# Two-block transformer kernel: the subtractions that split the modulation sums go from GpSimd to VectorE, half of an input split goes from VectorE to ScalarE, and the probabilities of differential attention are transposed one step later

## The chip, the cores and the metric

The kernel runs on one core of a Trainium2 chip. The metric is the device time of one launch in microseconds (us). Five engines work beside each other, each through its own queue in order: TensorE (PE in the profile, with its weight loads as PEld), VectorE (DVE), ScalarE (ACT), GpSimd (POOL) and SyncE (SP), which issues the transfers. An instruction that waits holds up all that stands behind it in its engine's queue.

## The reference, cut to what matters

The reference takes 256 tokens of 1024 features in fp32 through a first block (a SwiGLU feed-forward, a mixing layer of retention and neighbourhood attention, a second SwiGLU) and then through a second block of two layers. What the change touches lies in the second block:

```
mod = jnp.einsum('bd,lde->lbe', jax.nn.silu(c), ada_w) + ada_b[:, None, :]
for i in range(DEPTH_2):
    shift1, scale1, gate1, shift2, scale2, gate2 = jnp.split(mod[i], 6, axis=-1)
    h = x * (1.0 + scale1) + shift1
    y = moba_attention(h, ...) if i == 0 else diff_attention(h, ...)
    x = layer_norm(DEEPNORM_ALPHA * x + (1.0 + gate1) * y, ...)
    h = x * (1.0 + scale2) + shift2
    y = jnp.square(jax.nn.relu(h @ w_up)) @ w_down
    x = layer_norm(DEEPNORM_ALPHA * x + (1.0 + gate2) * y, ...)
# diff_attention, per head:  w = softmax(q1 k1^T) - lam * softmax(q2 k2^T);  o = rms_norm(w @ v)
```

`mod` is 12 vectors of 1024 numbers (two layers, six each). They depend on `c` alone and can be summed long before they are used.

## The kernel before, in words

**Weights as a stream.** All products with weights are made in fp32 precision from three products of a narrower form: a weight tile `raw` is split into an upper part `wh`, copied by ScalarE (L115), and a rest `wl = raw - wh`, subtracted by VectorE (L93). A pair of tiles is a slot of the stream, one tile of 128x1024 a piece. `tick` (L403 to L430) is called after each piece that TensorE has used up; it splits the next piece or two and then advances the background generators (`bg`), each of which runs up to its next `yield n` and sleeps n ticks. A generator's place on each engine's queue is thus fixed when the program is written. The stream keeps at most eight split pieces and six raw ones; SyncE's transfers are issued in the order of the stream.

**Modulation sums.** The weight `ada_w` comes as pieces of the same stream; the slots behind which they stand come from the table `at` (L310 to L314). Each of the 12 sums takes eight steps on VectorE (L335, L338) into `adacc`; partitions are not yet summed. Then `ada_parts` (L345 to L357) splits the sum into three bf16 parts: ScalarE copies (L348), GpSimd subtracts (L350), ScalarE copies (L352), GpSimd subtracts (L354). When the parts are there, `spare` sums them over the partitions by small matmuls in a PSUM bank that the hidden layer leaves free.

**Inputs.** `turn_of` (L584 to L608) transposes the normalized input on TensorE, scales and shifts it on ScalarE (`hf`, L602), and splits it on VectorE: an upper part (L606, listed as CAST) and the rest (L607). It is called for the first 128 tokens (t = 0) and the second (t = 1). While TensorE works on columns of the first, VectorE goes on to normalize the second (L646 to L659).

**Attention.** `attention.pair` is the generator of a head: scores `as` on TensorE, exponentials `P` on ScalarE (L1253), for layer 1 the difference of the two softmaxes on VectorE (L1263 to L1267), then the transposition `at` (L1276), its copy `T` on ScalarE (L1277), the product `ao` with the values, the head's norm `o` (L1308 to L1314) and its transposition (L1318). Rotation of q and k (L1223 to L1227) is emitted from the same ticks.

Of the kernel before, what the change touches and what calls it, by code (L numbers as in the profile page):

```python
# [9 lines left out]
F32 = mybir.dt.float32  # L10
F32R = mybir.dt.float32r
BF16 = mybir.dt.bfloat16
AF = mybir.ActivationFunctionType
OP = mybir.AluOpType
# [157 lines left out]
def block_kernel(ctx, tc, A, out):  # L172
    nc = tc.nc
    V, SC, PE, GP = nc.vector, nc.scalar, nc.tensor, nc.gpsimd
# [4 lines left out]
    work = ctx.enter_context(tc.tile_pool(name="work", bufs=1))  # L179
# [113 lines left out]
    for l, (wi, wo) in enumerate((("moba_w_in", "moba_w_out"), ("diff_w_in", "diff_w_out"))):  # L293
# [5 lines left out]
        for i in range(4):  # L299
# [6 lines left out]
    adas = [(l, s, i) for l, s in ((0, 0), (0, 1), (0, 3), (0, 4), (1, 0), (0, 2), (0, 5), (1, 1), (1, 3), (1, 4), (1, 2),  # L306
                                   (1, 5)) for i in range(4)]
    at = {}
    o = 0
    for n, g in ((nffn, 3), (nmix, 2), (nffn, 3), (natt, 0), (nmlp, 3), (natt, 0), (nmlp, 1)):  # L310
        for i in range(4 * g):
            a = 6 if o else 10
            at.setdefault(o + a + int((i // 4 + 0.2 * (i % 4)) * (n - a - 5) / g), []).append(adas.pop(0))
        o += n  # L314
    assert not adas
    for n, w in enumerate(ws):
# [28 lines left out]
    def ada_parts(l, s, t):  # L345

        parts = [adap[-1].tile([128, D], BF16, name=f"ada{i}", bufs=1) for i in range(3)]
        SC.activation(parts[0], t, AF.Copy)  # L348
        yield 1
        GP.tensor_tensor(t, t, parts[0], OP.subtract)  # L350
        yield 2
        SC.activation(parts[1], t, AF.Copy)  # L352
        yield 1
        GP.tensor_tensor(parts[2], t, parts[1], OP.subtract)  # L354
        yield 2
        ada_now.clear()
        ada_out.append((l, s, parts, None if s in (2, 5) else 0))  # L357

# [220 lines left out]

    def squares(s, src):  # L580

        SC.activation(work.tile([128, 512], F32, name="junk"), src, AF.Square, accum_out=s)

    def turn_of(src, a, c, alloc=gu):  # L584

        def turn(t):
            ps = [alloc("xt"), alloc("xt")]
            for k in range(8):
                PE.transpose(ps[k // 4][:, k % 4 * 128:k % 4 * 128 + 128], src[:, t, k * 128:(k + 1) * 128], ident)
            if c is None:  # L590
                for i in range(4):
                    for b in range(2):
                        k = 4 * b + i
                        x, h, l = ps[b][:, i * 128:(i + 1) * 128], XX[:, k, 0, TS[t]], XX[:, k, 1, TS[t]]
                        SC.activation(h, x, AF.Copy, scale=a[:, k:k + 1])
                        V.scalar_tensor_tensor(l, x, a[:, k:k + 1], h.bitcast(F32), op0=OP.mult, op1=OP.subtract)  # L596
                return
            for b in range(2):
                f = w2("hf")
                for i in range(4):  # L600
                    k = 4 * b + i
                    SC.activation(f[:, i * 128:(i + 1) * 128], ps[b][:, i * 128:(i + 1) * 128], AF.Identity,  # L602
                                  scale=a[:, k:k + 1], bias=c[:, k:k + 1])
                h, l = (XX[:, 4 * b:4 * b + 4, i, TS[t]] for i in range(2))
                f = f.rearrange("p (k s) -> p k s", k=4)
                V.tensor_copy(h, f)  # L606
                V.tensor_tensor(l, f, h.bitcast(F32), OP.subtract)  # L607
        return turn  # L608

# [605 lines left out]
    def attention(l, turn, after, mid):  # L1215
        with tc.tile_pool(name=f"att{l}", bufs=1) as mp:
# [13 lines left out]
            def pair(j, q, k):  # L1230
# [20 lines left out]
                for a in range(2):  # L1251
                    for c, sl in ((0, slice(0, 128)), (1, slice(128, 384))):
                        SC.activation(P[:, a, sl], ps[a][:, sl], AF.Exp, bias=mx[:, a, c:c + 1], scale=0.125,  # L1253
                                      accum_out=ss[:, c, a:a + 1])
# [5 lines left out]
                else:  # L1260
# [5 lines left out]
                    for c, sl in ((0, slice(0, 128)), (1, slice(128, 384))):  # L1266
                        V.scalar_tensor_tensor(P[:, 0, sl], P[:, 1, sl], lr[:, c:c + 1], P[:, 0, sl],  # L1267
                                               op0=OP.mult, op1=OP.add)
                yield 1
                nh = 2 - l  # L1270
                yield from room(nh)
                T = mp.tile([128, nh, 384], F32, name="T", bufs=2 + l)
# [211 lines left out]
```

## Time and profile before

| | |
|---|---|
| median of 3 runs | 1317.36 us (1317.07 to 1321.57) |
| the profiled execution's own time | 1319.84 us |
| its span, first to last instruction | 1318.0 us |
| TensorE busy | 1258.1 us, 95% |
| VectorE busy | 932.2 us, 71% |
| ScalarE busy | 642.8 us, 49% |
| GpSimd busy | 94.6 us, 7% |
| mean granted TensorE clock | 0.983 of full speed |

An execution takes 1.84 us more than its span. The stages in order are: FFN1 from about 8 to 210 us, the mixing layer to 440, FFN2 to 650, the first attention to 775, the first MLP to 965, differential attention to 1112, and the second MLP to the end. In the rows below, a line such as L93 is a line of the kernel before; a number in brackets is how long the engine idled ahead of the instruction, and what ended that; "x2" are two instructions of a kind in one row, with the time from the start of the first to the end of the last.

### The profile page before, as it was taken

The numbers are of one execution on the slowest core, as the hardware profiler recorded it, in microseconds if no ns is written. First come the engines' busy times: TensorE is split into PE (matmuls) and PEld (weight loads), VectorE is DVE, ScalarE is ACT, GpSimd is POOL, SyncE is SP. The second block draws the span as 40 slices with busy tenths as digits, with TensorE's granted clock in tenths as the row PEclk, the third lists the DMA queues.
The fourth block names the chain that finished last, engine by engine and source line by source line (L and its number), as shares of the span: only waits on it lengthen the run. The fifth ranks groups of instructions, "written<-read, shape, count | busy, mean of one in ns | idle before, by whom it ended". The sixth has DMA issues, their size and how long they took to land. (4 is left out here: it accounts for less than half of the span.)

```text
span 1318.0 us, 18965 instructions
## 1 busy us (share of the span) xinstructions
PE 1258.1 (95%) x7217; PEld 1073.1 (81%) x7222; DVE 932.2 (71%) x1276; ACT 642.8 (49%) x1032; POOL 94.6 (7%) x69
## 2 busy tenths in 40 slices
PE   9999899999999999999999999999899889999996
PEld 7877677888888878778789978988878777899885
DVE  5687576888676677667577667768677976775655
ACT  6543355545454454445455544435444544643540
POOL 0010010222000001001000000101100001000100
PEclk9999999999999999999999999999999999999998
DMA  9778687866576477878554336877665333576650
GB/s 305 258 250 278 212 258 168 261 212 193 190 223 205 145 249 236 290 258 266 171 181 137 112 118 215 266 256 262 221 231 176 113 109 126 175 249 222 223 192 32
DMA packets 167884, 271.68 MB, mean 206 GB/s; under 512 B 15888, under 2 KB 119664, under 8 KB 167792
## 3 DMA queue, kind: packets, MB, share of 16 engines
q1 hardware_dynamic: 161328, 268.36, 62.9%
q10 hardware_dynamic: 6464, 2.10, 1.0%
q8 instruction: 57, 0.93, 0.3%
q14 instruction: 35, 0.29, 0.1%
HBM read 269.37 MB, written 1.05 MB: 205 GB/s over the span
## 5 line engine op out<-in xcount | busy, mean ns | idle before, releaser
L93 DVE TENSOR_TENSOR wl<-raw,wh 128x1024 fp32r<-128x1024 f32 x392 | 487.9, 1273 | 58.2 <-ACT wh L115 57.0
L115 ACT ACTIVATE wh<-raw 128x1024 fp32r<-128x1024 f32 x392 | 399.7, 1055 | 161.7 <-issue 29.2
L201 PE MATMUL acc<-wh,H 128*128 128x512 f32 x864 | 286.5, 399 | 1.5 <-ACT wh L115 1.5
L201 PE MATMUL g<-wh,XX 128*128 128x512 f32 x832 | 268.3, 397 | 2.0 <-DVE XX L596 1.6
L201 PEld LDWEIGHTS acc<-wh,H 128*128 128x128 f32 x864 | 163.7, 189 | 43.2 <-issue 3.0
L201 PEld LDWEIGHTS g<-wh,XX 128*128 128x128 f32 x832 | 158.4, 190 | 37.5 <-DVE XX L596 2.0
L201 PE MATMUL acc<-wl,H 128*128 128x512 f32 x432 | 173.2, 401 | 1.5 <-DVE wl L93 1.5
L201 PE MATMUL g<-wl,XX 128*128 128x512 f32 x416 | 164.6, 396 | 5.2 <-DVE wl L93 5.2
L201 PE MATMUL u<-XX,wh 128*128 128x256 f32 x896 | 163.9, 284 | 1.5 <-ACT wh L115 1.5
L201 PEld LDWEIGHTS u<-XX,wh 128*128 128x128 f32 x896 | 142.2, 193 | 4.2 <-ACT wh L115 1.9
L201 PE MATMUL u<-XX,wl 128*128 128x256 f32 x448 | 127.5, 285 | 2.9 <-DVE wl L93 2.9
L338 DVE SCALAR_TENSOR_TENSOR adacc<-raw,csil,adacc 128x1024 f32<-128x1024 f32 x84 | 107.4, 1279 | 0.8
L201 PEld LDWEIGHTS g<-wl,XX 128*128 128x128 f32 x416 | 79.3, 191 | 23.2 <-DVE wl L93 7.1
L201 PEld LDWEIGHTS acc<-wl,H 128*128 128x128 f32 x432 | 82.0, 190 | 19.2 <-DVE wl L93 2.1
L201 PEld LDWEIGHTS u<-XX,wl 128*128 128x128 f32 x448 | 86.5, 193 | 3.3 <-DVE wl L93 3.3
L774 ACT ACTIVATE q<-u 128x512 f32<-128x512 f32 x28 | 16.8, 600 | 122.0 <-PE u L201 122.0
L775 DVE TENSOR_TENSOR q<-q,u 128x512 f32<-128x512 f32 x28 | 19.2, 686 | 80.0 <-ACT q L774 79.9
L711 ACT ACTIVATE a<-g,r 128x256 f32<-128x256 f32 x44 | 20.4, 474 | 93.4 <-PE g L201 93.4
L350 POOL TENSOR_TENSOR adacc<-adacc,ada 128x1024 f32<-128x1024 f32 x12 | 25.8, 2152 | 551.6 <-ACT ada L348 494.1
L713 DVE SCALAR_TENSOR_TENSOR b<-g,r,a 128x256 f32<-128x256 f32 x44 | 20.7, 481 | 58.0 <-ACT a L711 57.9
L201 PE MATMUL v<-wh,XX 128*128 128x256 f32 (+1 forms) x192 | 49.4, 344 | 5.1 <-DVE XX L606 5.1
L201 PE MATMUL q<-XX,wh 128*128 128x256 f32 x256 | 47.4, 286 | 0.0
(289 smaller groups left out, 1818.4 us busy)
## 6 DMA issues: line engine op xcount, KB each, us to landing
raw<-in_ada_w_dram SPq DMA_DIRECT2D x96, 512.0 KB, 5.2
raw<-in_ffn_w_in_dram SPq DMA_DIRECT2D x176, 256.0 KB, 5.0
raw<-in_mlp_w_up_dram SPq DMA_DIRECT2D x64, 512.0 KB, 4.8
raw<-in_mlp_w_down_dram SPq DMA_DIRECT2D x64, 512.0 KB, 4.8
raw<-in_w_mix_in_dram SPq DMA_DIRECT2D x52, 512.0 KB, 4.8
raw<-in_ffn_w_out_dram SPq DMA_DIRECT2D x44, 512.0 KB, 5.7
raw<-in_moba_w_in_dram SPq DMA_DIRECT2D x24, 512.0 KB, 4.7
raw<-in_diff_w_in_dram SPq DMA_DIRECT2D x24, 512.0 KB, 4.8
```

The costliest lines, as they stand in the source:

```text
L93: self.nc.vector.tensor_tensor(wl, raw, wh.bitcast(F32), OP.subtract)
L115: nc.scalar.activation(wh, raw, AF.Copy)
L201: PE.matmul(o, l, r, start=start, stop=stop, skip_group_check=True)
L338: V.scalar_tensor_tensor(t, w, csil[:, kb:kb + 1], t, op0=OP.mult, op1=OP.add)
L350: GP.tensor_tensor(t, t, parts[0], OP.subtract)
L711: SC.activation(two(a)[:, t], ps[t][:, 0:256], AF.Silu, scale=r[0][:, t:t + 1])
L713: V.scalar_tensor_tensor(two(b)[:, t], ps[t][:, 256:512], r[0][:, t:t + 1], two(a)[:, t], op0=OP.mult, op1=OP.mult)
L774: SC.activation(q, p, AF.Relu)
L775: V.tensor_tensor(q, q, p, OP.mult)
```

## The change

Five edits:

- In the table `at` the pieces of a stage's sums are spread over two slots more (`n-a-3` for `n-a-5`), so that most stand zero to three slots later than before.
- Both subtractions of `ada_parts` go from GpSimd to VectorE (24 instructions of 128x1024), and each is followed by a pause of one tick and not two.
- The output of `squares`, which nobody reads, is bf16.
- In `turn_of`, with a shift and for t = 0, the upper part is copied by ScalarE and not VectorE; four inputs, two copies each.
- In `pair`, for layer 1 and heads 0 to 5, the pause ahead of the transposition is two ticks and not one.

```diff
-            at.setdefault(o + a + int((i // 4 + 0.2 * (i % 4)) * (n - a - 5) / g), []).append(adas.pop(0))
+            at.setdefault(o + a + int((i // 4 + 0.2 * (i % 4)) * (n - a - 3) / g), []).append(adas.pop(0))
...
         SC.activation(parts[0], t, AF.Copy)
         yield 1
-        GP.tensor_tensor(t, t, parts[0], OP.subtract)
-        yield 2
+        V.tensor_tensor(t, t, parts[0], OP.subtract)
+        yield 1
         SC.activation(parts[1], t, AF.Copy)
         yield 1
-        GP.tensor_tensor(parts[2], t, parts[1], OP.subtract)
-        yield 2
+        V.tensor_tensor(parts[2], t, parts[1], OP.subtract)
+        yield 1
...
-        SC.activation(work.tile([128, 512], F32, name="junk"), src, AF.Square, accum_out=s)
+        SC.activation(work.tile([128, 512], BF16, name="junk"), src, AF.Square, accum_out=s)
...
-                V.tensor_copy(h, f)
+                if t:
+                    V.tensor_copy(h, f)
+                else:
+                    SC.activation(h, f, AF.Copy)
                 V.tensor_tensor(l, f, h.bitcast(F32), OP.subtract)
...
-                yield 1
+                yield 1 + (l == 1 and j < 6)
                 nh = 2 - l
```

Behind line 583 the lines of the changed kernel have numbers higher by one to three (L711 is L714, L1276 is L1279).

**First place: ScalarE in FFN1, around the second modulation sum.** `a` is the hidden layer's activation of one slot, two instructions; `ada0` and `ada1` are the parts of the sum; each `wh` is one piece of weights. Before:

```order
L711 ACTIVATE a_1260<-g_1172,r_297 128x256
L711 ACTIVATE a_1260<-g_1173,r_297 128x256
L115 ACTIVATE wh_1266<-raw_1190 128x1024
L115 ACTIVATE wh_1273<-raw_1206 128x1024
L352 ACTIVATE ada1_1210<-adacc_961 128x1024
L545 ACTIVATE H_1304<-g_1172 128x2x256
L115 ACTIVATE wh_1361<-raw_1244 128x1024
L115 ACTIVATE wh_1364<-raw_1270 128x1024
L711 ACTIVATE a_1417<-g_1347,r_297 128x256
L711 ACTIVATE a_1417<-g_1348,r_297 128x256
L115 ACTIVATE wh_1423<-raw_1298 128x1024
L115 ACTIVATE wh_1426<-raw_1344 128x1024
```

The changed kernel, from the copy of the sum's first part on:

```order
L348 ACTIVATE ada0_1235<-adacc_961 128x1024
L714 ACTIVATE a_1251<-g_1175,r_297 128x256
L714 ACTIVATE a_1251<-g_1176,r_297 128x256
L115 ACTIVATE wh_1257<-raw_1151 128x1024
L115 ACTIVATE wh_1260<-raw_1173 128x1024
L115 ACTIVATE wh_1280<-raw_1196 128x1024
L115 ACTIVATE wh_1285<-raw_1213 128x1024
L352 ACTIVATE ada1_1236<-adacc_961 128x1024
L545 ACTIVATE H_1296<-g_1175 128x2x256
L115 ACTIVATE wh_1311<-raw_1216 128x1024
L115 ACTIVATE wh_1317<-raw_1232 128x1024
L115 ACTIVATE wh_1374<-raw_1289 128x1024
```

In the first list the pair `a_1417` stands ahead of the piece `wh_1423`. In the second no pair stands behind `wh_1257`, but the pair `a_1251` now stands ahead of it, and `wh_1257` is the first piece behind the copy L348.

**Second place: TensorE and VectorE in differential attention, around the transposition of one head's P.** `q` and `k` are projections of other heads, `at` the transposition, `ao` the head's product and, from L1318 (L1321), the transposition of `o`. TensorE before:

```order
L201 MATMUL k_9487<-XX_73,wl_9312 128x256
L1318 MATMUL ao_9593<-cst_74,o_9597 128x128 x2
L1276 MATMUL at_9717<-cst_74,P_9605 128x128 x3
L201 MATMUL q_9729<-XX_73,wh_9364 128x256 x2
L201 MATMUL q_9729<-XX_73,wl_9365 128x256
L201 MATMUL q_9729<-XX_73,wh_9364 128x256 x2
```

TensorE in the changed kernel:

```order
L201 MATMUL q_9719<-XX_73,wl_9365 128x256
L1321 MATMUL ao_9645<-cst_74,o_9649 128x128 x2
L1279 MATMUL at_9756<-cst_74,P_9590 128x128 x3
L201 MATMUL as_9764<-k_9695,q_9562 128x128
L201 MATMUL as_9765<-k_9695,q_9562 128x128
L201 MATMUL as_9764<-k_9695,q_9562 128x256
```

The transposition `at` of a head stood ahead of the piece of q; now a whole piece of q has gone by, and the next head's scores `as` follow it. VectorE before, from the norm `o` of one head to the rotation of k:

```order
L1312 TENSOR_TENSOR r_9603<-r_9603,rs_9479 128x2
L1314 TENSOR_SCALAR o_9597<-ao_9593,r_9603 128x128 x2
L1263 RECIPROCAL lr_9665<-ss_9539 128x2
L1264 RECIPROCAL rs_9664<-ss_9539 128x2
L1265 SCALAR_TENSOR_TENSOR lr_9665<-lr_9665,lam_86,ss_9539 128x2
L1267 SCALAR_TENSOR_TENSOR P_9605<-P_9605,lr_9665 128x128
L1267 SCALAR_TENSOR_TENSOR P_9605<-P_9605,lr_9665 128x256
L1223 STREAM_SHUFFLE sh_9700<-k_9487 128x512
L1225 TENSOR_TENSOR k_9702<-k_9487,cst_74 128x512
L1226 TENSOR_TENSOR sh_9700<-sh_9700,cst_74 128x512
L1227 TENSOR_TENSOR k_9702<-k_9702,sh_9700 128x512
```

VectorE in the changed kernel:

```order
L1268 SCALAR_TENSOR_TENSOR lr_9658<-lr_9658,lam_86,ss_9521 128x2
L1270 SCALAR_TENSOR_TENSOR P_9590<-P_9590,lr_9658 128x128
L1270 SCALAR_TENSOR_TENSOR P_9590<-P_9590,lr_9658 128x256
L1226 STREAM_SHUFFLE sh_9693<-k_9481 128x512
L1228 TENSOR_TENSOR k_9695<-k_9481,cst_74 128x512
L1229 TENSOR_TENSOR sh_9693<-sh_9693,cst_74 128x512
L1230 TENSOR_TENSOR k_9695<-k_9695,sh_9693 128x512
L93 TENSOR_TENSOR wl_9638<-raw_9368,wh_9637 128x1024
L1328 SCALAR_TENSOR_TENSOR Y_9041<-ao_9572,sm_82,Y_9041 128x256
L1315 TENSOR_TENSOR r_9655<-r_9655,rs_9473 128x2
L1317 TENSOR_SCALAR o_9649<-ao_9645,r_9655 128x128 x2
```

The norm `o` stood ahead of the next head's difference of softmaxes; now it stands behind it, behind the rotation of k, a `wl` and a `Y`.

**Third place: ScalarE at the input of the first MLP, first tokens.** Before:

```order
L658 ACTIVATE v_7037<-v_7037,nm_7078,r_7076 128x512
L602 ACTIVATE hf_7113<-xt_7103,m00c_6931,m00a_6930 128x128 x4
L602 ACTIVATE hf_7120<-xt_7104,m00c_6931,m00a_6930 128x128 x4
L115 ACTIVATE wh_7133<-raw_6904 128x1024
L115 ACTIVATE wh_7136<-raw_6955 128x1024
L115 ACTIVATE wh_7139<-raw_6991 128x1024
```

The changed kernel:

```order
L661 ACTIVATE v_7037<-v_7037,nm_7078,r_7076 128x512
L602 ACTIVATE hf_7113<-xt_7103,m00c_6931,m00a_6930 128x128 x4
L609 ACTIVATE XX_73<-hf_7113 128x4x128
L602 ACTIVATE hf_7120<-xt_7104,m00c_6931,m00a_6930 128x128 x4
L609 ACTIVATE XX_73<-hf_7120 128x4x128
L115 ACTIVATE wh_7133<-raw_6904 128x1024
L115 ACTIVATE wh_7136<-raw_6955 128x1024
L115 ACTIVATE wh_7139<-raw_6991 128x1024
```

Each copy to XX stands behind its four instructions for `hf`; the second four start behind the first copy, and the pieces of weights behind both.

## Rows read from the trace of the kernel before

**Rows 1.** Page, part 1: busy time of each engine, share, instructions.

```profile
PE 1258.1 (95%) x7217; PEld 1073.1 (81%) x7222; DVE 932.2 (71%) x1276; ACT 642.8 (49%) x1032; POOL 94.6 (7%) x69
```

**Rows 2.** Waits of TensorE, FFN1 (80 to 180 us): waiter, released by: us, times, longest.

```profile
PE g L201 <- DVE wl L93: 5.2, 5, 1.9
PE g L201 <- POOL ada L354: 2.9, 1, 2.9
PE acc L201 <- ACT wh L115: 1.5, 1, 1.5
```

**Rows 3.** Waits of TensorE, FFN2 (540 to 580 us).

```profile
PE g L201 <- POOL ada L354: 2.7, 1, 2.7
```

**Rows 4.** Waits of TensorE, first MLP (880 to 940 us).

```profile
PE u L201 <- DVE wl L93: 2.9, 2, 1.9
PE u L201 <- ACT wh L115: 1.5, 1, 1.5
```

**Rows 5.** Waits of TensorE, input of the first MLP (775 to 792 us).

```profile
PE u L201 <- DVE XX L606: 2.5, 2, 2.3
```

**Rows 6.** Waits of TensorE, differential attention (1015 to 1090 us).

```profile
PE at L1276 <- DVE P L1267: 6.0, 6, 1.7
```

**Rows 7.** Groups of instructions, GpSimd: busy us, mean ns, idle before.

```profile
L354 POOL TENSOR_TENSOR ada<-adacc,ada 128x1024 bf16<-128x1024 f32 x12 | 32.0, 2663 | 81.9 <-ACT ada L352 81.9
L350 POOL TENSOR_TENSOR adacc<-adacc,ada 128x1024 f32<-128x1024 f32 x12 | 25.8, 2152 | 551.6 <-ACT ada L348 494.1 <-issue 57.5
```

**Rows 8.** Timeline of FFN1 (124 to 128 us): start, us, instruction, idle before and releaser.

```profile
124.08 0.62 PE L201 MATMUL g<-wh,XX 128*128 128x512 f32 x2
...
124.46 2.14 POOL L350 TENSOR_TENSOR adacc<-adacc,ada 128x1024 f32<-128x1024 f32 x1 [28.55 <-ACT ada L348]
...
125.30 3.52 DVE L93 TENSOR_TENSOR wl<-raw,wh 128x1024 fp32r<-128x1024 f32 x2 [2.08 <-ACT wh L115]
...
127.73 0.50 PE L201 MATMUL g<-wl,XX 128*128 128x512 f32 x1 [1.92 <-DVE wl L93]
```

**Rows 9.** Timeline of FFN1 (154.5 to 158.5 us).

```profile
157.13 0.51 PE L201 MATMUL acc<-wh,H 128*128 128x512 f32 x1 [1.51 <-ACT wh L115]
...
158.39 0.50 PE L201 MATMUL acc<-wl,H 128*128 128x512 f32 x1 [0.76 <-DVE wl L93]
```

**Rows 10.** Windows: stretch (FFN1), us, busy of PE, PEld, DVE, ACT, POOL, clock, DMA, GB/s.

```profile
30.00:210.00 180.00, 169.12 (x796) 135.93 (x795) 123.46 (x155) 81.70 (x101) 14.28 (x6) 0.98 0.77 253
```

**Rows 11.** Timeline of the input of the first MLP (783 to 790 us).

```profile
782.88 0.43 DVE L606 CAST XX<-hf 128x512 fp32r<-128x512 f32 x1 [0.24 <-ACT hf L602]
...
783.96 0.68 DVE L646 TENSOR_TENSOR v<-oacc,grow 128x512 f32<-128x512 f32 x1
...
787.38 0.82 ACT L658 ACTIVATE v<-v,nm,r 128x512 f32<-128x512 f32 x1 [1.68 <-DVE nm L657]
```

**Rows 12.** Groups of instructions, ScalarE, shapes apart.

```profile
L545 ACT ACTIVATE H<-q 128x512 fp32r<-128x512 f32 x28 | 17.4, 621 | 5.3 <-DVE q L775 5.3
```

**Rows 13.** Timeline of differential attention (1044.5 to 1053 us).

```profile
1045.74 0.61 DVE L1314 TENSOR_SCALAR o<-ao,r 128x128 f32<-128x128 f32 x2
...
1047.22 0.74 PE L1276 MATMUL at<-cst,P 128*128 128x128 f32 x3 [0.37 <-DVE P L1267]
...
1047.39 0.73 DVE L1223 STREAM_SHUFFLE sh<-k 128x512 f32<-128x512 f32 x1
...
1047.72 0.48 PE L201 MATMUL q<-XX,wh 128*128 128x256 f32 x2
...
1048.00 0.49 ACT L1277 ACTIVATE T<-at 128x384 f32<-128x384 f32 x1 [0.64 <-PE at L1276]
...
1049.94 1.22 DVE L93 TENSOR_TENSOR wl<-raw,wh 128x1024 fp32r<-128x1024 f32 x1
...
1050.67 0.83 PE L201 MATMUL ao<-vt,T 128*128 128x128 f32 x6
1051.07 0.47 DVE L1325 SCALAR_TENSOR_TENSOR Y<-ao,sm,Y 128x256 fp32r<-128x256 f32 x1
```


## The prediction, made before the changed kernel was run

> **What bounds the kernel now.** I read the busy times first: TensorE is at work for 95% of the span, VectorE for 71%, ScalarE for 49%, GpSimd for 7% [rows 1]. So the sum of TensorE's work sets the time, and this change leaves that work alone. What it can win or lose are the holes in TensorE's row. For them I read the waits of TensorE, stage by stage, and then the timeline around the long ones. The reader should see in the waits that the holes which touch this change are few and named: in FFN1 5.2 us on `wl`, 2.9 on GpSimd's L354 and 1.5 on `wh` [rows 2]; in FFN2 2.7 on L354 [rows 3]; in the first MLP 2.9 on `wl` and 1.5 on `wh` [rows 4]; at the input of the first MLP 2.5 on the split input [rows 5]; in differential attention 6.0 on the combined P [rows 6].
>
> **Subtractions on VectorE.** GpSimd takes 2.15 us for the first and 2.66 us for the second subtraction of a sum, twelve of each [rows 7]. VectorE has not done this form with this output, but `wl` is a subtraction of two 128x1024 operands too: 1.22 us where nothing runs on GpSimd [rows 13]. Beside a GpSimd subtraction the row of two `wl` takes 3.52 us [rows 8], that is 3.52 - 1.22 = 2.30 for the one that GpSimd slows. I take 1.22 us a piece; the ends are 0.73, VectorE's shuffle of half as many columns [rows 13], and 2.66, GpSimd's own time. So VectorE gets 24 x 1.22 = 29.3 us of new work, and gets back up to 24 x (2.30 - 1.22) = 25.9 us, if every GpSimd subtraction slowed one `wl`. The net, some 3 us, lies in VectorE's idle time: 180.0 - 123.5 = 56.5 us in FFN1 alone [rows 10]. If that cover is missing, each subtraction costs TensorE up to 1.22 us; that is the third rival. A subtraction waits for ScalarE's copy, and behind it in VectorE's queue wait the next `wl` and accumulations, and TensorE for those. The copy stands a tick ahead, so I take this wait at nothing.
>
> **Order in FFN1.** What goes: the `wl` waits of rows 2, of which the one at 127.73 us (1.92) is a `wl` slowed beside L350 [rows 8]; the wait of `spare` on L354 (2.9), since five ticks take the place of seven and 1.22 us that of 2.66; and the pair at 157 us, where `wh` stood behind two activations and TensorE waited 1.51 for it and 0.76 for its `wl` [rows 9]. That is 5.2 + 2.9 + 1.5 + 0.8 = 10.4 us. What comes: the order shows the same placing of `wh` behind two activations at two other slots, priced like that pair, 2.3 us each; and at the third sum the copy L348, which waits for the last accumulation, now stands ahead of a `wh` that TensorE needs next, which I price at the same 2.3. So 6.8 us come back, between 0 (the pieces were early enough) and 8 (L348's copy adds a microsecond). Net -3.6.
>
> **FFN2 and the first MLP.** The wait on L354 goes (2.7) [rows 3]; in the MLP the order puts the pieces that waited ahead of L348, so 2.9 + 1.5 = 4.4 go [rows 4]. I see nothing that takes their place, since the sums are spread over two slots more. SyncE's issues follow the stream, so an `ada_w` piece that moves by a slot or two moves its transfer past the weights of those slots, six raw pieces ahead as before; I take that at nothing. Net -7.1; at the worst half of it is found elsewhere as a wait on `wl`. The table's later slots in the mixing layer and the second MLP meet no wait of TensorE that I know of; nothing. The bf16 output of `squares`: nothing.
>
> **The copy on ScalarE.** Before, the second CAST starts at 782.88 us, takes 0.43, the rest follows, and VectorE begins with the second tokens (L646) at 783.96 [rows 11]. On ScalarE a copy from SBUF of 128x512 with this output takes 0.62 us [rows 12]. The second four `hf` start 0.62 later, the second copy takes 0.62 for 0.43, and VectorE's own second subtraction starts behind it: 0.62 + 0.62 - 0.43 = 0.81 us later than today. From there a chain without slack runs over L646 to the second tokens' input, on which TensorE waits 2.5 us today [rows 5]. So the wait grows by 0.81, at four inputs: +3.2. With a copy of 0.43 a site costs 0.43, with 0.82 (ScalarE's scaled pass over 512 columns) [rows 11] 1.21: +1.7 to +4.8; and nothing where the chain is not the last. What would hide it is not there: TensorE already waits. The Trainium skill, Perfetto Trace Analysis, Optimizing Scalar/DVE Operations, says that of work which either engine can do VectorE is quicker where it has a performance mode, and that moving it to ScalarE may make sense where VectorE is saturated. The trace agrees (0.43 against 0.62 us), and VectorE at 71% is not saturated; by that rule this edit is a loss, as in my sum, and an edit that cost nothing would make the total 3.2 better.
>
> **Differential attention.** With one tick more, P is finished long before its transposition, and the six waits on P go: -6.0 [rows 6]. A wait of another kind comes. VectorE's `o` now stands behind the rotation of k, a `wl`, a `Y`. The rotation can start when k is there, when TensorE reaches the end of that piece. From there: rotation 1049.94 - 1047.39 = 2.55, `wl` 1.22, Y 0.47, the norm's factor and `o` 0.15 (an estimate, a very short instruction) + 0.61: 5.0 us. TensorE has in that time a piece of q, 1050.67 - 1047.72 = 2.95, and the other head's 0.3: a wait of 1.75 for `o` [rows 13]. The order shows this for two heads: +3.5, between 0 and 5. And two scores take a PSUM bank that the head's `at` has just left; they wait for the copy T: it started 0.64 after `at` and takes 0.49, against an `at` of 0.74 [rows 13], some 0.75 with the hand-over each: +1.5. Net -1.0, between -6.0 and +2.
>
> **Restarts.** A hole costs more than its idle time: a matmul behind it takes 0.50 us, where back to back two take 0.62 from first start to last end [rows 8], 0.39 of it the second: 0.23 apart. So 0.27 us for each hole. Gone: 8 in FFN1, 1 in FFN2, 3 in the MLP, 6 in attention; come: 6 and 4. 8 fewer: -2.2.
>
> **Sum.** -3.6 - 7.1 + 3.2 - 1.0 - 2.2 = -10.7 us against the profiled execution's 1319.84, its span of 1318.0 with 1.84 around it: 1309.1. That execution is 2.5 us over the median of the three runs, 1317.36; the change applied to the median gives 1306.7.
>
> **Rivals.** *More is won.* The new waits in FFN1 and attention don't come, since the pieces are ahead: 6.8 + 5.0 with 10 restarts (2.7) fewer, -25 in all: about 1292; half of it 1299. For it speaks that TensorE waits rarely; against it that the order places the same instructions as at 157 us. *Waits only move.* FFN1 nets nothing, FFN2 and the MLP win half (-3.5), attention nets +1, the inputs cost 3.2, restarts nothing: +0.7, and about 1317. For it: VectorE is in order and every hole in the list is one on a late VectorE or ScalarE. Against it: FFN2's and the MLP's waits hang on GpSimd's time, which is gone. *Slower: the subtractions take the lead that `wl` has.* Place: VectorE's queue right behind each of the 24. Price: 1.22 us each, at most 29.3. Only the gains of moved waits stand against it; with -10.7 as the rest, it decides from (10.7 + 6.6) / 1.22 on, 15 of the 24; all of them would give 1336.0. Against it: VectorE has 31% free in FFN1 [rows 10]. *GpSimd is not what slows `wl`.* Then the 25.9 us don't come back and VectorE has 29 more; the waits at `wl` (5.2 + 2.9) stay: -10.7 + 8.1 = -2.6: 1314.8. Against it rows 8, where the slow one is the one beside L350. The Trainium skill, GPSIMD Engine Reference, Key points, says that GpSimd shares its SBUF interfaces with VectorE's instructions of two SBUF inputs; the trace agrees (2.30 against 1.22 us), and that rival's chance is small by it.
>
> **Numbers.** Below and above 0.5%, 6.6 us, is about what a measurement can tell from no change: 1310.8 to 1323.9. Forecast (its own range 1301 to 1312) 0.58; more won 0.14; waits move 0.16; slower 0.07; GpSimd not the cause 0.05. Faster: nearly all of the first two, 0.70; same 0.23, of which 0.02 come from the forecast's upper end; slower 0.07. The range of 1298 to 1317 leaves out half of "more is won", the slower one and a little of "waits move".
>
> **What would show it.** Right: no POOL row of 128x1024; mean `wl` near 1.22 us; no wait of TensorE on L354 or on P for heads 0 to 5; waits on XX longer by 0.8 at the four inputs; two waits on `o` of about 1.75; in FFN1 two waits for `wh` behind activations. Wrong: waits of TensorE on `wl` right after L350 or L354 on VectorE, a VectorE subtraction well over 1.3 us, or waits for `ada_w` transfers.

## The result, and the profile after

The changed kernel takes 1306.96 us, the median of 4 runs (1305.18 to 1309.30), against 1318.17 for the kernel before with one more run taken beside it; the ratio is 0.989 (95% interval 0.987 to 0.992). In a later group of runs it took 1305.79 against 1321.31, ratio 0.987 (0.985 to 0.990). So it is 11 to 16 us faster by the medians. The prediction was 1306.7 with a range of 1298 to 1317.

The profiled execution took 1307.54 us, span 1305.7, 12.3 us less than before. Its busy times, part 1 of the page:

```profile
PE 1253.8 (96%) x7216; PEld 1072.5 (82%) x7222; DVE 930.8 (71%) x1292; ACT 644.8 (49%) x1040; POOL 36.9 (3%) x45
```

Against [rows 1] TensorE has about the same work, VectorE is no busier than before although it has 16 instructions more (24 subtractions came, eight copies left), and GpSimd's share is down to 3%. Of the 12.3 us, 8.0 are idle time of TensorE (59.9 to 51.9 us of the span) and 4.3 its busy time for the same work. The reader should look at VectorE first: the prediction had +3 us net for the subtractions. With the eight copies taken away as well VectorE is 1.4 less busy; in the kernel without the copy edit, run below, it is at 932.6, 0.4 more than before. The groups of VectorE's instructions (busy us, mean ns, idle before) say why:

```profile
L93 DVE TENSOR_TENSOR wl<-raw,wh 128x1024 fp32r<-128x1024 f32 x392 | 468.5, 1222 | 49.5 <-ACT wh L115 47.9 <-DMA raw<-in_ffn_w_in_dram 0.6 <-DMA raw<-in_ffn_w_out_dram 0.5
...
L350 DVE TENSOR_TENSOR adacc<-adacc,ada 128x1024 f32<-128x1024 f32 x12 | 14.6, 1217 | 0.0
L354 DVE TENSOR_TENSOR ada<-adacc,ada 128x1024 bf16<-128x1024 f32 x12 | 14.6, 1216 | 0.0
```

Both subtractions take 1.22 us, the value taken from the undisturbed `wl` in [rows 13], and the mean of all `wl` fell from 1273 to 1222 ns: 392 of them give 19.4 us back; the subtractions of `H` from `q` (L546) give another 3.4 (22.6 to 19.1 us).

Where the 12.3 us come from can be read from when TensorE starts the first product of each stage (start times in us of those rows of the timeline):

| stage | starts before | starts after | length before | length after | difference |
|---|---|---|---|---|---|
| FFN1 | 7.59 | 8.04 | 208.68 | 204.53 | -4.1 |
| mixing | 216.27 | 212.57 | 197.16 | 197.52 | +0.4 |
| FFN2 | 413.43 | 410.09 | 242.98 | 237.87 | -5.1 |
| first attention | 656.41 | 647.96 | 125.56 | 125.10 | -0.5 |
| first MLP | 781.97 | 773.06 | 201.34 | 194.05 | -7.3 |
| differential attention | 983.31 | 967.11 | 135.72 | 137.44 | +1.7 |
| second MLP | 1119.03 | 1104.55 | 188.72 | 190.33 | +1.6 |

The second MLP's length goes to the start of the last product; the rest is 0.45 at the start and 0.5 behind it. A stage's length holds the waits for its successor's input too. Single executions of the same stage differ by up to 2.7 us: FFN1 has the same instructions in the change and in three kernels below that undo other edits, and took 204.5 and 204.4 (the change, twice), 204.6 (without the copy), 203.5 (without the pause) and 206.2 (without both). The mixing layer ends at 413 us and FFN2 at 656, and not at the 440 and 650 given ahead of the prediction.

Now the waits of TensorE that answer to [rows 2 to 6], in the changed kernel. FFN1, 80 to 185 us:

```profile
PE acc L201 <- ACT wh L115: 3.0, 2, 1.5
PE g L201 <- ACT wh L115: 1.8, 1, 1.8
PE acc L201 <- DVE wl L93: 1.5, 2, 0.8
PE g L201 <- DVE wl L93: 0.8, 1, 0.8
PE g L201 <- DVE ada L354: 0.4, 1, 0.4
```

The waits of [rows 2] are gone, the five on `wl`, the one on L354 but for 0.4 us, and the pair at 157 us. In their place stand three pairs, `wh` and then its `wl`: two of 1.5 + 0.8 and one of 1.8 + 0.8, where the prediction had three of 2.3. In FFN2 and in the first MLP, the stretches that answer to [rows 3, 4] hold no such wait any more. At the input of the first MLP:

```profile
PE u L201 <- DVE XX L607: 2.3, 1, 2.3
PE xt L589 <- ACT v L661: 1.2, 2, 1.0
```

The wait on XX of [rows 5] is as long as before; the 0.8 us came out as a longer wait of the transposition on `v`, of up to 1.0, which is the same chain one step earlier. In differential attention, against [rows 6]:

```profile
PE ao L1321 <- DVE o L1317: 5.2, 3, 1.9
PE as L201 <- ACT T L1280: 2.2, 3, 1.0
PE as L201 <- DVE k L1230: 1.5, 1, 1.5
```

No wait of the transposition on P is left, and the scores' wait on the exponentials P, 2.1 us before, is 0.3. Three on `o`, of up to 1.9, three on the copy T and one on the rotated k stand there. The third on `o`, of 1.4 at the end of the stage, is an old one: it stood behind the stretch of [rows 6] with 1.0.

One of the new pairs in FFN1, in ScalarE's queue (start, us, instruction, idle before):

```profile
129.22 0.47 ACT L714 ACTIVATE a<-g,r 128x256 f32<-128x256 f32 x1 [2.98 <-PE g L201]
130.51 0.47 ACT L714 ACTIVATE a<-g,r 128x256 f32<-128x256 f32 x1 [0.82 <-PE g L201]
130.89 3.89 ACT L115 ACTIVATE wh<-raw 128x1024 fp32r<-128x1024 f32 x4
```

and on TensorE:

```profile
130.09 0.39 PE L201 MATMUL g<-wh,XX 128*128 128x512 f32 x1
131.99 0.50 PE L201 MATMUL acc<-wh,H 128*128 128x512 f32 x1 [1.51 <-ACT wh L115]
133.25 0.50 PE L201 MATMUL acc<-wl,H 128*128 128x512 f32 x1 [0.76 <-DVE wl L93]
133.59 0.86 PE L201 MATMUL acc<-wh,H 128*128 128x512 f32 x2
```

The four `wh` start at 130.89, behind both activations; TensorE is through with all it had at 130.5 and gets the first `wh` at 131.99. It is the picture of [rows 9], at another slot.

### The profile page after: what moved, and what is told of

It is laid out like the page before. It is cut to its first block, busy times and chain, and to the rows that moved or that the text cites. A ratio compares the mean times of both kernels' runs of the same rounds, so it can differ in the third digit from the quotient of the medians.

```text
span 1305.7 us, 18953 instructions
## 1 busy us (share of the span) xinstructions
PE 1253.8 (96%) x7216; PEld 1072.5 (82%) x7222; DVE 930.8 (71%) x1292; ACT 644.8 (49%) x1040; POOL 36.9 (3%) x45
## 5 line engine op out<-in xcount | busy, mean ns | idle before, releaser
L93 DVE TENSOR_TENSOR wl<-raw,wh 128x1024 fp32r<-128x1024 f32 x392 | 468.5, 1222 | 49.5 <-ACT wh L115 47.9
L115 ACT ACTIVATE wh<-raw 128x1024 fp32r<-128x1024 f32 x392 | 398.0, 1053 | 148.4 <-issue 22.5
L201 PEld LDWEIGHTS g<-wh,XX 128*128 128x128 f32 x832 | 158.5, 190 | 38.7 <-ACT wh L115 2.3
L201 PEld LDWEIGHTS acc<-wl,H 128*128 128x128 f32 x432 | 81.6, 189 | 19.1 <-DVE wl L93 2.1
L777 ACT ACTIVATE q<-u 128x512 f32<-128x512 f32 x28 | 16.8, 599 | 119.1 <-PE u L201 119.1
L714 ACT ACTIVATE a<-g,r 128x256 f32<-128x256 f32 x44 | 20.5, 473 | 89.4 <-PE g L201 89.4
L201 PE MATMUL k<-XX,wh 128*128 128x256 f32 x256 | 47.3, 286 | 0.0
```

The lines of the kernel that those rows point to most:

```text
L93: self.nc.vector.tensor_tensor(wl, raw, wh.bitcast(F32), OP.subtract)
L115: nc.scalar.activation(wh, raw, AF.Copy)
L201: PE.matmul(o, l, r, start=start, stop=stop, skip_group_check=True)
L714: SC.activation(two(a)[:, t], ps[t][:, 0:256], AF.Silu, scale=r[0][:, t:t + 1])
L777: SC.activation(q, p, AF.Relu)
```

## The experiments

Twelve runs. Each time stands beside the kernel before on the same chip; that kernel's median was 1321.0 to 1321.7 in all four groups, so times of different groups can be compared to about a microsecond.

| kernel | time us (lowest to highest) | ratio to before (95%) |
|---|---|---|
| the change without the copy on ScalarE | 1302.33 (1300.40 to 1305.44) | 0.986 (0.984 to 0.988) |
| the change without the longer pause | 1308.80 (1308.33 to 1310.16) | 0.991 (0.990 to 0.992) |
| the change without both | 1304.62 (1302.11 to 1306.44) | 0.988 (0.986 to 0.989) |
| before, subtractions on VectorE, pauses of one | 1308.13 (1304.15 to 1309.71) | 0.990 (0.988 to 0.991) |
| the change again | 1305.79 (1304.25 to 1308.40) | 0.987 (0.985 to 0.990) |
| before, later slots alone | 1306.46 (1304.40 to 1309.39) | 0.988 (0.985 to 0.990) |
| before, subtractions on VectorE, pauses of two | 1310.13 (1307.30 to 1314.58) | 0.991 (0.988 to 0.993) |
| the change with GpSimd at work beside it | 1317.93 (1312.24 to 1322.20) | 0.996 (0.995 to 0.998) |
| later slots in FFN1, without the copy | 1290.24 (1289.88 to 1291.67) | 0.977 (0.975 to 0.980) |
| the same, without the longer pause | 1294.45 (1289.43 to 1295.94) | 0.980 (0.977 to 0.983) |
| the same, longer pause for heads 0, 2, 4 | 1297.40 (1293.19 to 1301.07) | 0.982 (0.979 to 0.985) |
| before, all the later slots, GpSimd subtracts | 1294.98 (1293.84 to 1296.46) | 0.980 (0.978 to 0.982) |

**The copy on ScalarE.** Undone alone:

```diff
-                if t:
-                    V.tensor_copy(h, f)
-                else:
-                    SC.activation(h, f, AF.Copy)
+                V.tensor_copy(h, f)
```

> The changed kernel with the upper part for t = 0 back on VectorE (CAST at all eight places), all else as changed. Theory (the copy on ScalarE lengthens a chain without slack): VectorE starts with the second tokens 0.8 us earlier at each of four inputs, the wait of the transposition xt on v shrinks by 0.8 us there, and the time is 3.2 us under the changed kernel's 1306.96, about 1303.8. Rival (the chain has slack, or ScalarE was in the way elsewhere): no difference, 1306 to 1308.

The changed kernel itself was run beside the next group:

> The changed kernel itself, on the same chip as the next three, to compare with. Theory (its gain is in TensorE's holes): 10 to 14 us under the kernel before on this chip too. Rival (part of the first gain was that chip's clock): under 8.

It was 15.5 us under the kernel before. Without the copy it is 1302.33 us, 3.5 under the change's 1305.79. The theory holds. All waits of the transposition on `v`, over the whole program, in the changed kernel and then without the copy:

```profile
PE xt L589 <- ACT v L661: 4.0, 5, 1.0
```

```profile
PE xt L589 <- ACT v L658: 1.1, 3, 0.6
```

4.0 us in five places become 1.1 in three.

**The longer pause in attention.** Undone alone, and with the copy:

```diff
-                yield 1 + (l == 1 and j < 6)
+                yield 1
```

> The changed kernel with the pause ahead of the transposition of P back at one tick, all else as changed. Theory (the waits only changed places: in the trace the holes of TensorE in differential attention, its input's left out, are 13.8 us before and 14.2 after): the six waits on P are back (6.0 us), the waits on o and on the copy T are gone, and the time is within 1 us of the changed kernel, 1306 to 1308. Rival (the edit is worth what the waits on P held): 6 us slower, about 1313.

> The changed kernel with both of those edits undone: only VectorE's subtractions with their pauses of one tick, the later slots and the bf16 output are left. Theory (the gain is all in the modulation sums, and the two edits cost 3.2 and about 0): 3.5 us under the changed kernel, about 1303.5. Rival (each of the two edits carries some of the gain): over 1308.

Without the pause 1308.80, 3.0 over the change; without both 1304.62, 2.3 over the kernel without the copy alone. Both the expected "within 1 us" and the 6 us of the rival are wrong: the pause is worth 2 to 3 us. That the two edits hold opposite signs, and that the gain lies in the sums, stands. What the pause gains is not seen in the idle time; how far it is in the granted clock is asked below.

**Engine or slots.** The edit of the engine alone, on the kernel before:

```diff
-        GP.tensor_tensor(t, t, parts[0], OP.subtract)
-        yield 2
+        V.tensor_tensor(t, t, parts[0], OP.subtract)
+        yield 1
...
-        GP.tensor_tensor(parts[2], t, parts[1], OP.subtract)
-        yield 2
+        V.tensor_tensor(parts[2], t, parts[1], OP.subtract)
+        yield 1
```

> The kernel before with both subtractions on VectorE and pauses of one tick, the slots as before. Theory (GpSimd's time and its slowing of wl were the cause of the holes in the feed-forward stages): the two waits on L354 (5.6 us) go and the waits on wl in FFN1 and the first MLP shrink by over half; FFN1, FFN2 and the first MLP together 10 us shorter, time about 1308. Rival (the later slots take the holes away, not the engine): no more than 6 us gained, 1312 or more.

1308.13, 13.3 under the kernel before; the time is as expected, and the rival falls. Of the two waits on L354 that were to go, though, one of 2.0 us is left. The waits of TensorE in FFN1 and in the first MLP of this kernel:

```profile
PE g L201 <- DVE wl L93: 2.4, 4, 0.8
PE g L201 <- DVE ada L354: 2.0, 1, 2.0
PE acc L201 <- ACT wh L115: 1.5, 1, 1.5
```

```profile
PE u L201 <- DVE wl L93: 1.7, 2, 1.0
PE u L201 <- ACT wh L115: 1.5, 1, 1.5
```

The `wl` waits of [rows 2] are halved, not gone, and in the MLP of [rows 4] 3.2 of 4.4 us are left, those on `wl` less than halved: VectorE is quicker, but `wh` and `wl` still come late. The slots alone, on the kernel before:

```diff
-            at.setdefault(o + a + int((i // 4 + 0.2 * (i % 4)) * (n - a - 5) / g), []).append(adas.pop(0))
+            at.setdefault(o + a + int((i // 4 + 0.2 * (i % 4)) * (n - a - 3) / g), []).append(adas.pop(0))
```

> The kernel before with the later slots alone (GpSimd still subtracts, pauses of two). Theory (the holes beside the sums have two causes, GpSimd's time and the place of L348 ahead of the needed weights; the slots cure the second alone, mostly in the first MLP): 2 to 5 us under the kernel before; mean wl stays near 1270 ns; waits on L354 stay. Rival (slots alone do it): 8 us or more. Other rival (slots do nothing without the engine): within 1 us.

1306.46, 14.9 under the kernel before. The theory of 2 to 5 us falls, and its first rival, that the slots alone do it, has the right size. FFN1 of this kernel:

```profile
PE acc L201 <- ACT wh L115: 3.0, 2, 1.5
PE g L201 <- ACT wh L115: 1.8, 1, 1.8
...
PE g L201 <- POOL ada L354: 1.3, 1, 1.3
```

In FFN1 it has the same three pairs as the changed kernel, the last with a wait of 1.9 on its `wl` for 0.8, which ends at 185.57, and its length is that of before (208.66 us, from 8.74 to 217.40). TensorE idles 9.6 us of it where it idled 10.9, but the granted clock over the stage is 0.96 where it was 0.98; in the first MLP no wait is left and 9.1 us go, in FFN2 5.2. The engine alone takes 4.2 from FFN1, 5.4 from FFN2 and 2.2 from the MLP (first products at 8.13, 212.63, 409.85, 647.46, 772.05 and 971.15). So in FFN2, and in part in the MLP, the two edits are two cures of the same waits, and together they give little more than either: 13.3 and 14.9 apart, 16.8 together (1304.62). The bf16 output of `squares`, which is in the last of these times, was not run alone; its instructions take 628 and 594 ns, 629 and 600 before.

The pauses, on the same kernel as the engine alone:

```diff
         V.tensor_tensor(t, t, parts[0], OP.subtract)
-        yield 1
+        yield 2
...
         V.tensor_tensor(parts[2], t, parts[1], OP.subtract)
-        yield 1
+        yield 2
```

> The kernel before with both subtractions on VectorE, but with the pauses of two ticks and the slots as before. Theory (the engine is the cause, the ticks only make room for the slower engine): mean wl 1222 ns, waits on L354 gone since it is done long before, and about the same time as with pauses of one, 12 to 13 us under the kernel before. Rival (the saved ticks count): 5 us slower than with pauses of one.

1310.13, 2.0 over pauses of one, with ranges that overlap; the saved ticks count for little, if at all. The expectation had no wait on L354 left; there are three, 4.3 us in all and up to 2.0.

**GpSimd beside VectorE.** Added to the changed kernel, ahead of each subtraction on VectorE (the tile `scr` is read by nobody):

```diff
+        for i in range(2):
+            GP.tensor_tensor(scr[0], cst[:, 512 * i:512 * i + 512], parts[0][:, 512 * i:512 * i + 512], OP.subtract)
         V.tensor_tensor(t, t, parts[0], OP.subtract)
```

> The changed kernel with GpSimd working again beside it: for each of the 24 subtractions it also subtracts the fresh part from a constant into a tile that nobody reads, in two halves of 512 columns, so that nothing waits for it. Theory (GpSimd's traffic slows VectorE's two-operand subtractions): mean wl back to 1260 to 1275 ns, and as nothing waits for GpSimd only the slowed wl and subtractions count: VectorE 20 to 45 us busier, time 2 to 6 us over the changed kernel. Rival (the slow wl had another cause, such as ScalarE's copies of the sum): mean wl 1222 ns and the same time.

1317.93, 12.1 over the change, more than the theory's 2 to 6. GpSimd's groups, and of the page its busy times and the `wl`:

```profile
L358 POOL TENSOR_TENSOR scr<-cst,ada 128x512 bf16<-128x512 f32 x24 | 42.5, 1772 | 47.4 <-ACT ada L355 46.4
L352 POOL TENSOR_TENSOR scr<-cst,ada 128x512 bf16<-128x512 f32 x24 | 34.5, 1439 | 561.8 <-ACT ada L349 503.7 <-issue 57.1
```

```profile
PE 1255.2 (95%) x7216; PEld 1071.4 (81%) x7222; DVE 957.8 (73%) x1292; ACT 646.0 (49%) x1040; POOL 114.0 (9%) x93
...
L93 DVE TENSOR_TENSOR wl<-raw,wh 128x1024 fp32r<-128x1024 f32 x392 | 482.8, 1259 | 46.9 <-ACT wh L115 46.1
```

GpSimd works 77.0 us here, more than the 57.8 of [rows 7], so the price is not that of the old subtractions one to one. But nothing waits for it, the mean `wl` is back at 1259 ns, and VectorE is 27.0 us busier than in the changed kernel with the same instructions. So GpSimd does slow VectorE beside it, and with the new instructions on VectorE that costs time.

**The order in FFN1.** The three pairs left are, as I read the order of the changed kernel, pieces that ScalarE splits only one piece ahead of their use. Spreading FFN1's pieces by two slots more leaves no such piece:

```diff
-            at.setdefault(o + a + int((i // 4 + 0.2 * (i % 4)) * (n - a - 3) / g), []).append(adas.pop(0))
+            at.setdefault(o + a + int((i // 4 + 0.2 * (i % 4)) * (n - a - (3 if o else 1)) / g), []).append(adas.pop(0))
```

This stands on the kernel without the copy.

> The changed kernel without the copy on ScalarE, and with FFN1's pieces of the sums spread by two slots more (n-a-1 in FFN1 alone), where the order shows no wh any more that is split only one piece ahead of its use. Theory (the holes left in FFN1, 3.0 + 1.8 us on wh and 1.5 + 0.8 on its wl, hang on that order alone): they go, FFN1 some 7 us shorter than without the copy alone, 1302.3 - 7 = about 1295. Rival (the later sums bring their own holes into the end of FFN1): 1299 or more.

1290.24, 12.1 under the kernel without the copy: the theory's direction, and 5 us more than its size. It is 15.6 under the change and 31 under the kernel before (0.977, 0.975 to 0.980). The one wait left in FFN1, and the window of 80 to 185 us (busy of PE, PEld, DVE, ACT, POOL; granted clock; share of the transfers; GB/s) of this kernel:

```profile
PE g L201 <- DVE ada L354: 1.9, 1, 1.9
```

```profile
80.00:185.00 105.00, 103.15 (x504) 84.61 (x504) 79.29 (x102) 48.84 (x60) 0.00 (x0) 1.00 0.81 266
```

and the same window of the changed kernel:

```profile
80.00:185.00 105.00, 97.43 (x459) 78.22 (x458) 76.38 (x97) 46.97 (x58) 0.00 (x0) 0.97 0.77 247
```

Two numbers differ: TensorE is busy 5.7 us longer in the same 105 us, and its clock is 1.00 where it was 0.97 (it is 0.97 without the copy, too). The second number is not as sure as the first: of the two kernels below with the same FFN1, one has 1.00 in this window and the other 0.98, and FFN1 takes 193.1 us in the one and 197.1 in the other, with 2.0 us idle in both.

The pause on this kernel, first one tick for all heads as shown above, then:

```diff
-                yield 1 + (l == 1 and j < 6)
+                yield 1 + (l == 1 and j in (0, 2, 4))
```

> The same with the pause ahead of the transposition of P back at one tick. Theory (waits on P of 6.0 us against waits on o, T and k of about the same size): within 1.5 us of the kernel with the pause of two. Rival (the pause is worth the 2 us by which the two pairs of earlier runs differ): 2 to 3 us slower than with it.

> The same with the pause of two ticks for heads 0, 2 and 4 alone. Theory (the waits on o belong to heads 1 and 3, whose delay puts the next head's difference of softmaxes and the rotation of k ahead of their o): the two waits of 1.9 us on o go, waits on P for heads 1, 3 and 5 come back with about 1.3, 1.3 and 1.7 us, so within 1.5 us of the kernel with all six. Rival (delaying every second head makes neighbours meet): 3 us slower.

Without the pause 1294.45, 4.2 slower: the rival's direction and more than its size, though the ranges overlap. With the pause at three heads alone 1297.40, 7.2 slower, the theory falls, and the rival's mechanism is in the trace. TensorE's transpositions in that kernel:

```profile
1005.04 0.49 PE L1276 MATMUL at<-cst,P 128*128 128x128 f32 x3
1009.46 0.74 PE L1276 MATMUL at<-cst,P 128*128 128x128 f32 x3 [3.93 <-DVE P L1267]
```

The delayed transposition of one head and the undelayed one of the next now meet with no product between them, and VectorE has the rotation of k, a `wl` and a pass over X to do before the second P. There are three such waits, 8.6 us in all; with no pause there are 4.9 us in five, and 4.3 were expected. The profiled execution was the slowest of the five, and the ranges with three pauses and with none overlap, so how much worse it is than no pause at all is not sure.

At last the slots alone, on the kernel before, with GpSimd:

```diff
-            at.setdefault(o + a + int((i // 4 + 0.2 * (i % 4)) * (n - a - 5) / g), []).append(adas.pop(0))
+            at.setdefault(o + a + int((i // 4 + 0.2 * (i % 4)) * (n - a - (3 if o else 1)) / g), []).append(adas.pop(0))
```

> The kernel before with the slots alone: n-a-1 in FFN1 and n-a-3 elsewhere; GpSimd still subtracts, no other edit. Theory (place and engine are separate causes: the slots free the wh pieces, the engine takes the slowing of wl and its long wait): 1296 to 1302, that is 2 to 8 us over the same slots with VectorE's subtractions (1294.45) and 4 or more under the first spread with GpSimd (1306.46). Rival (with the right slots the engine makes no difference): 1293 to 1295. Other rival (GpSimd's slowing of wl fills the freed time again): 1306 or more.

1294.98 against 1294.45 with VectorE's subtractions on the same slots: the rival, that the engine makes no difference, holds. FFN1's waits of this kernel and its `wl`:

```profile
PE g L201 <- POOL ada L354: 2.1, 1, 2.1
PE g L201 <- DVE wl L93: 0.5, 1, 0.5
```

```profile
L93 DVE TENSOR_TENSOR wl<-raw,wh 128x1024 fp32r<-128x1024 f32 x392 | 487.6, 1273 | 56.5 <-ACT wh L115 55.8
```

`wl` is as slow as in the kernel before (1273 ns), and one wait of 0.5 us is all that it does in FFN1. A slowed `wl` costs time only where it is the last one ready.

**The clock behind a wait.** Windows of the changed kernel around the first pair in FFN1 (columns as above):

```profile
120.00:130.00 10.00, 10.00 (x46) 8.26 (x45) 5.38 (x6) 1.53 (x2) 0.00 (x0) 1.00 0.96 327
130.00:133.25 3.25, 0.98 (x5) 0.25 (x3) 1.98 (x4) 2.73 (x4) 0.00 (x0) 1.00 0.23 74
133.25:136.50 3.25, 3.25 (x9) 2.58 (x10) 3.25 (x3) 2.47 (x3) 0.00 (x0) 0.58 0.55 161
136.50:139.50 3.00, 3.00 (x15) 2.44 (x14) 0.86 (x3) 1.40 (x2) 0.00 (x0) 0.88 0.87 233
...
173.00:177.00 4.00, 4.00 (x21) 3.26 (x20) 2.34 (x4) 0.60 (x1) 0.00 (x0) 1.00 0.85 233
...
182.50:186.50 4.00, 4.00 (x13) 3.16 (x13) 4.00 (x4) 4.00 (x5) 0.00 (x0) 0.69 0.85 280
```

Before the pair the granted clock is 1.00. Behind it, it is 0.58 over 3.25 us, close to the lower of its two levels, 1.2 of 2.4 GHz, and then comes back. In that window 9 matmuls are counted, in 3.00 us of the next 15. Behind the second pair, from 173 us, it stays at 1.00, and behind the third, from 182.5 us, it is 0.69. So a slow stretch can follow a wait, and need not. In the kernel before it is so behind the wait on L354 in FFN2 [rows 3], which ended at 570.1 us:

```profile
570.00:574.00 4.00, 3.93 (x11) 3.09 (x11) 2.54 (x3) 2.12 (x2) 0.02 (x1) 0.58 0.95 304
574.00:578.00 4.00, 3.95 (x19) 2.93 (x18) 0.00 (x0) 1.06 (x1) 0.00 (x0) 1.00 0.85 284
```

At 0.58 of the clock 4 us do the work of 2.3, so this wait cost 2.7 us and 1.7 more. With the 0.27 of a restart that is 4.7 of the 5.1 us that FFN2 gained.

The same stretch stands behind the pair in the first MLP before (0.79 over 937 to 945 us, that is 1.7 us again) and is gone after. But there the changed kernel loses 1.7 us more behind its input, where the copy on ScalarE lengthened the wait: 0.66 over 780 to 790 us, against 0.83 over the ten microseconds that answer to them before. Over the whole span the granted clock is 0.983 before and 0.980 after, so on balance, in these two executions, the change did not win by the clock.

For the pause in attention the whole stage has to be laid beside the whole stage. Differential attention and the second MLP on the later slots, with the pause and then without:

```profile
955.20:1091.98 136.78, 122.35 (x824) 106.54 (x825) 105.96 (x226) 67.17 (x170) 8.45 (x10) 0.95 0.42 131
1091.98:1279.09 187.11, 184.80 (x1123) 163.37 (x1126) 120.64 (x139) 82.23 (x105) 1.53 (x2) 1.00 0.58 190
```

```profile
953.95:1091.56 137.61, 123.64 (x825) 107.48 (x825) 105.85 (x226) 67.83 (x170) 8.45 (x10) 0.95 0.43 131
1091.56:1280.29 188.73, 186.42 (x1124) 164.51 (x1126) 120.65 (x139) 82.22 (x105) 1.53 (x2) 0.99 0.58 188
```

With the pause the stage is 0.8 us shorter at the same clock, though TensorE idles 0.5 us longer in it; the second MLP, with the same instructions, is 1.6 shorter at 1.00 than at 0.99. The pair without the copy says the same: 136.70 and 137.60 at 0.95, then 187.10 at 1.00 and 188.72 at 0.99. In the changed kernels the stage itself differs, 0.95 and 0.96 in two executions with the pause and 0.94 without; but the kernel before, without any pause, has 0.97 in it. So the clock may hold a part of what the pause gains, in good part behind the stage; what makes the stage itself shorter is not shown. These are single executions, and no run set the clock apart from the waits, so this stays a reading.

## Why the prediction was right, point by point

**Bound.** TensorE's work is unchanged; the gain came out of its waits. Right in the main: of the 12.3 us, 8.0 are idle time, and 4.3 are busy time (1258.1 to 1253.8), for which the sum had the restarts, 2.2.

**Subtractions on VectorE.** 1.22 us each: 1.217 and 1.216. Net on VectorE +3: 0.4 with the copies left where they were. But for the 0.4 us on L354 no wait behind a subtraction was seen; the third rival did not come. But the reason given for the FFN1 term, that the slowing of `wl` by GpSimd makes the waits, is half of it: the last experiment keeps the slowing and has hardly a wait.

**Order in FFN1.** Three new pairs at 2.3: 2.27, 2.27 and 2.60 (1.84 + 0.76). Net -3.6, with a restart or two about -4.1: the stage's length is 4.1 us shorter. The pairs were read rightly from the order. That the length fits to half a microsecond is in part luck, since five executions of this stage spread over 2.7 us.

**FFN2 and the first MLP.** -7.1 and 4 restarts of 0.27: about -8.2; the stages are 5.1 and 7.3 shorter, 12.4 together, although the MLP's holds a longer wait at its input. This term was mis-sized: the 0.27 for a restart left out the lower clock that can follow a wait, 1.7 us behind the one in FFN2 and 1.7 behind the pair in the MLP, where the input took it back; and [rows 4] left out a wait of 0.7 of `acc` on `wl` in the same stretch, which went too. That nothing would take the place of those waits was right.

**The copy.** +3.2: undoing it gave 3.5. Right, at the step said, though the longer wait shows at the transposition at three of the inputs and at XX, 2.55 for 1.89, only at the first attention's.

**Differential attention.** The waits on `o` were predicted at two heads with 1.75 us: 1.9. The rows of VectorE and TensorE at the first of them:

```profile
1033.39 1.22 DVE L93 TENSOR_TENSOR wl<-raw,wh 128x1024 fp32r<-128x1024 f32 x1
1034.52 0.48 DVE L1328 SCALAR_TENSOR_TENSOR Y<-ao,sm,Y 128x256 fp32r<-128x256 f32 x1
1034.92 0.15 DVE L1315 TENSOR_TENSOR r<-r,rs 128x2 f32<-128x2 f32 x1
1035.10 0.61 DVE L1317 TENSOR_SCALAR o<-ao,r 128x128 f32<-128x128 f32 x2
```

```profile
1035.77 0.44 PE L1321 MATMUL ao<-cst,o 128*128 128x128 f32 x2 [1.90 <-DVE o L1317]
```

`wl`, Y, the norm's factor and `o` follow the rotation just as the sum had them, and TensorE waits 1.90. The wait on T came at up to 1.0 for 0.75. Not named were a wait on the rotated k (1.5), 0.4 more on `o` at the end of the stage, and the 1.8 that the scores' wait on the exponentials lost. In the pairs with and without the pause TensorE idles 0.4 to 1.3 us more in the stage with it, for the -1.0 of the sum; the total time says -2.3 to -4.2 in the three pairs of kernels. The sign is right, but not for the reason given: the waits changed places and did not shrink. Where the gain comes from stays open; the clock may hold a part of it.

**Sum.** Predicted -10.7: -11.2 in the first runs, -15.5 in the later group. That the first of them fits to half a microsecond is luck, for the sum came out closer than its terms: in the profiled execution FFN2 and the MLP gave 4 us more than predicted, and differential attention and the second MLP gave 3.3 back, where the sum had little more than two inputs' copies (1.6) against a gain of 1.0.

**Rivals.** "Waits only move" was true of differential attention's idle time and not of the rest; its +0.7 on the median gives 1318, where the prediction has 1317. "GpSimd is not what slows `wl`" is excluded by the run with GpSimd beside. But the later slots with GpSimd show that this slowing need not cost anything. "More is won" did not come with this change, but its mechanism, FFN1 without the three pairs, is what the later slots gave: 12.1 us, where the prediction's 6.8 and 3 pairs of restarts (1.6) would have been 8.4.

## What to carry to other kernels

Where a tuned stream feeds TensorE, read for each weight piece how far ahead of its use it is split, and what stands ahead of it on the splitting engine: here three pieces split one piece ahead cost more than 24 slow subtractions on another engine. Two cures of one wait don't add up, so try each alone before crediting one; the spread of the slots with nothing else was worth as much as the five edits together. And give a wait of TensorE a second price, the slow stretch that can follow it: it was 1.7 us behind a wait of 2.7. As it follows some waits and not others, price it as a range, and compare whole stages in more than one execution before crediting an edit with it.

## What the runs showed of the hardware that was not expected

A wait of TensorE of about 2.3 us (1.51 + 0.76) was followed by 3.25 us at a granted clock of 0.58, another one of the same length by none. The same instructions of FFN1 on the later slots took 193.1 us at a clock of 1.00 in one execution and 197.1 at 0.98 in another, with the same 2.0 us of idle time. A subtraction of 128x512 from SBUF on GpSimd took 1.4 to 1.8 us in halves (1439 and 1772 ns), twice of which is 2.9 and 3.5 us, more than the 2.15 and 2.66 of one whole instruction [rows 7], though with another first operand and other work beside it (the quickest half took 1.16); beside them VectorE was 27.0 us busier with the same instructions. Without the three pairs the window of 80 to 185 us kept the full clock in two of three executions and had 0.98 in the third.
